# A decoder layer in fp32: modulation blocks that share accumulators, and weight units in pairs

## The chip, the core and the metric

The kernel runs on one core of one Trainium2 chip. The metric is the device time of one launch in microseconds (us), as the median of several runs. A core has a matrix engine (PE, with its weight loads shown apart as PEld), a vector engine (DVE), a scalar engine (ACT), GpSimd (POOL), and SyncE (SP), whose queue issues the weight transfers here. Each engine runs its own list of instructions in the order in which it was written, and semaphores tie the lists together.

## The reference

One layer of a decoder works on a prompt of 256 rows and on 8 x 4 sample rows, together T = 288 rows of D = 2048, all in fp32. A vector c for the prompt and one for each of the 8 samples (9 in all) gives the modulation:

```
sh_m, sc_m, gt_m, sh_f, sc_f, gt_f = split(silu(c) @ w_ada + b_ada, 6)
h = rmsnorm(x) * (1 + sc_m) + sh_m
q, k, v, gu, gv = split(h @ w_in)
merged = concat(rmsnorm(window_attention(q, k, v)), rmsnorm(gelu(gu) * mix(rmsnorm(gelu(gv)))))
x = x + gt_m * rmsnorm(merged @ w_out)
h = rmsnorm(x) * (1 + sc_f) + sh_f
x = x + gt_f * rmsnorm(square(relu(h @ w_ff1)) @ w_ff2)
```

`w_ada` is 2048 x 12288, `w_in` 2048 x 3328, `w_out` 2048 x 2048, `w_ff1` 2048 x 8192 and `w_ff2` 8192 x 2048. The keys, the values and the normalised rows of gv of the sample are outputs too.

## The kernel before

Activations lie transposed, features on the partitions. Each fp32 operand of a big product is the sum of two parts, h (the value rounded to the engine's shorter type) and l (the rest). A weight tile of 128 x 2048 raw values (1 MB) is loaded by SP (L306) into one of 5 buffers, ACT makes its h (CAST, L317) and DVE its l (L318), each in halves of 1024 columns. A product of 128 output columns (`Main`) is then 48 matmuls of 128 x 288: xh and xl against h (L332, L333) and xh against l (L336), twice over 8 tiles of the contraction. `Win` does the same for `w_in` (L478, L479, L481), but in seven groups of the contraction (`KG` of 1, 1, 2, 2, 2, 3 and 5 tiles), because only the part of h that has its modulation can be multiplied; after each group every column tile goes from PSUM to SBUF, by copies in the first group (L486 on ACT, L488 on DVE), by additions on DVE later (L490). `SlabK` (L897) holds several accumulators open and goes along the contraction.

`modnorm` makes one tile of the modulated input: for the 256 prompt rows one DVE instruction with the scale (L283), one ACT instruction with the shift that writes xh (L287) and one on DVE that writes xl (L289); for the 32 sample rows three small DVE instructions (L284, scale L285, shift L286), a CAST on ACT (L288) and xl (L291). `prep(g)` calls it for the tiles of group g ahead of the products of that group.

The modulation is worked out in 96 units of 1 MB of `w_ada`, which stand in 34 blocks (which of the six vectors, first tile, width w of 1, 2 or 4 tiles). A unit (`Ada.run`, L359) multiplies a 128 x 32 slice of the activated c (9 columns and zeros) with the raw weights in fp32, 16 / w matmuls that go around the four 32-row strips of one PSUM bank; each shows as two matmuls in the profile. After the last unit of a block, ACT copies the bank (adS, L363), `ada_fin` makes w transposes on PE (L371), and DVE reduces over the four strips (L373) and adds the bias (L381); a scale or gate is also multiplied with a gain (L383).

What sets the order: the items are written into one list, and `drive` runs it, loading 4 units ahead and splitting 1 ahead. `spread` mixes the ada units of group g+1 between the products of group g. In the attention the tables `NA_L` and `NA_A` say how many units `na` puts after each step, between the slabs of the output projection it is `NA_S`, between its products `NA_O`, and `NA_R` units are left for the residual. In the feed-forward stage the last vector (`Gf`) has one item of `adas2` after each product of the first layer with c > 0. A scheduler then sorts the instructions of each engine by priority and readiness, so that the true order of an engine is that of the built program, not of the list.

Of the kernel before, what the change touches and what calls it, by code (L numbers as in the profile page):

```python
# [62 lines left out]
def _order():  # L63
    res = []
    for g in range(len(KG)):
        res += _mix_blocks(g)
    res += [(2, 4 * q, 4) for q in range(4)]
    for q in range(4):
        res += [(4, 4 * q, 4), (3, 4 * q, 4)]
    return res + [(5, 4 * q, 4) for q in range(4)]  # L70


ADA_BLOCKS = _order()
# [32 lines left out]
def build():  # L106
# [32 lines left out]
    with tile.TileContext(nc) as tc, ExitStack() as root:  # L139
# [37 lines left out]
        cT = cp.tile([128, KT, 9], F32, name="cT")  # L177
# [4 lines left out]
        ones2 = cp.tile([128, 128], F32, name="ones2")  # L182
        eps = cp.tile([128, 1], F32, name="eps")
        mods = {n: cp.tile([128, KT, 9], F32, name="mod_" + n) for n in ("Am", "Bm", "Gm", "Af", "Bf", "Gf")}

# [10 lines left out]
        V.memset(ones2, 2.0 / D)  # L196
        V.memset(eps, EPS)

        sc = cp.tile([128, KT, 32], F32, name="sc")
# [5 lines left out]
        V.tensor_tensor(sc[:, :, 0:9], sg_, cT, ALU.mult)  # L205
# [12 lines left out]
        def norm_r(ps, name):  # L218
# [3 lines left out]
            exp_ln(r, ps, AF.Ln, bias=eps)  # L222
            V.tensor_scalar(a, ps, EPS, None, ALU.add)  # L223
            rsqrt(r, a, t, False)
            return r

        class Sumsq:
            def __init__(self, n, pe, w=None):
                self.n, self.pe, self.i = n, pe, 0
                self.w = ones if w is None else w  # L230
                if pe:
                    self.ps = pp.tile([128, 512], F32, name="ps")[:, :T]
# [6 lines left out]
            def add_sq(self, sq):  # L239
                if self.pe:  # L240
                    PE.matmul(self.ps, self.w, sq, start=self.i == 0, stop=self.i == self.n - 1)
# [16 lines left out]
            def open(self, stop):  # L258
                self.ps = pp.tile([128, 512], F32, name="ps")[:, :T]
                PE.matmul(self.ps, self.w, self.acc, start=True, stop=stop)  # L260

            def close(self, src):
# [3 lines left out]
                PE.matmul(self.ps, self.w, sq, start=False, stop=True)  # L266
# [75 lines left out]
        class Ada(Unit):  # L342
            nosplit = True

            def __init__(self, blk, i):
                self.c, self.j0, self.w = self.blk = blk
                self.i = i
                self.src = d_wada[ADA_ROW[blk] + i]

            def run(self):  # L350
                w, cw = self.w, 128 * self.w
                if self.i == 0:
                    st["ada", self.blk] = pa.tile([128, 512], F32, name="ada")
                ps = st["ada", self.blk]
                nk = KT // w
                for kk in range(nk):
                    k = self.i * nk + kk
                    g = 32 * (k % 4)
                    PE.matmul(ps[g:g + 32, :cw], sc[:, k], self.raws[:, kk * cw:kk * cw + cw], start=k < 4,  # L359
                              stop=k >= KT - 4, skip_group_check=True)  # L360
                if self.i == w - 1:
                    sb = cp.tile([128, 512], F32, name="adS", bufs=2)
                    S.copy(sb[:, :cw], ps[:, :cw])  # L363
                    st["ada", self.blk] = sb

        def ada_fin(blk):
            c, j0, w = blk
            sb = st["ada", blk]
# [3 lines left out]
            m = cp.tile([128, 4, 9], F32, name="adm", bufs=2)[:, :w]  # L372
            V.tensor_reduce(m, pt[:, :w * 128].rearrange("p (w g c) -> p w c g", w=w, g=4)[:, :, 0:9], AX.X, ALU.add)  # L373
            n = ADA[c]
            dst = mods[n][:, j0:j0 + w]

            def row(name, a):
                o_ = SMALL[name][0] + a
                return small[:, o_:o_ + w].unsqueeze(2).to_broadcast([128, w, 9])

            V.tensor_tensor(m if n in ADG else dst, m, row("bada", 16 * c + j0), ALU.add)  # L381
            if n in ADG:
                V.tensor_tensor(dst, m, row(ADG[n], j0), ALU.mult)  # L383

        def ada_items(blk):
            return [Ada(blk, i) for i in range(blk[2])] + [Do(ada_fin, blk)]
# [24 lines left out]
        # ---- norm of x  # L411
        first = []
        for b in _mix_blocks(0):
# [6 lines left out]
        def norm_x():  # L420
# [6 lines left out]
            st["rx"] = norm_r(s0.result(), "r_x")  # L427

        # ---- small tables
# [20 lines left out]
        # ---- startup: ada for mixing scale / shift and first 12 column tiles of W_in  # L450
# [49 lines left out]
        # ---- attention  # L500
# [136 lines left out]
        # ---- gMLP  # L637
# [87 lines left out]
        # ---- schedule: startup  # L725
        def prep(g):
            for k in range(KG0[g], KG0[g] + KG[g]):
                modnorm(k, st["rx"], mods["Am"], mods["Bm"])

# [12 lines left out]
        for g in range(len(KG) - 1):  # L742
            win = [Win(pc) for pc in WIN_PIECES if pc[0] == g]
            ada = []
            for b in _mix_blocks(g + 1):
                ada += ada_items(b)
            ada.append(Do(prep, g + 1))
            if g == GTAB:
                ada.append(Do(tables))
            if g == GSMP:  # L750
                ada.append(Do(samp0, 0))
            items += spread(win[:-1], ada) + win[-1:]

        def ssq_attn(i):
            if i == 0:
                st["sa"] = Sumsq(8, False, ones2)
            st["sa"].add(at[:, i])

        def rattn():
            st["ra"] = norm_r(st["sa"].result(), "r_a")  # L760

        def ssq_gate(h):
            if h == 0:
                st["sg"] = Sumsq(8, False, ones2)
# [7 lines left out]
        def rgate():  # L772
            st["rg"] = norm_r(st["sg"].result(), "r_g")

        adas = []
        for b in ADA_BLOCKS:
            if b[0] in (2, 3, 4):
                adas += ada_items(b)
        adas2 = []
        for b in ADA_BLOCKS:  # L780
            if b[0] == 5:
# [377 lines left out]
```

## Time and profile before

| | |
|---|---|
| time of the runs | 1332.75, 1334.24, 1335.09 us (median 1334.24) |
| profiled execution | span 1331.0 us |
| PE busy | 1298.7 us (98%) |
| DVE, ACT busy | 739.8 us (56%), 543.6 us (41%) |
| weight transfers | 291.41 MB, mean 219 GB/s |

The span runs from the first to the last instruction of the one profiled execution; the runs' times also hold what lies around it, some 3 us. PE is busy nearly throughout, so the time is first of all a sum of PE's work; where PE is idle, another engine's chain counts. The stages that the text speaks of: the start with the first groups of `w_in` (to 57 us), its groups 2 to 5 (to 188, by rounded limits), the last group with the attention (to 303), the gate and the first slabs of the output projection (to 345), its remaining products (to 453), the residual and the first slabs of the feed-forward part (to 515), and the feed-forward products (to 1314).

### The profile page before, as it was taken

The numbers are of one execution on the slowest core, as the hardware profiler recorded it, in microseconds if no ns is written. First come the engines' busy times: TensorE is split into PE (matmuls) and PEld (weight loads), VectorE is DVE, ScalarE is ACT, GpSimd is POOL, SyncE is SP. The second block draws the span as 40 slices with busy tenths as digits, with TensorE's granted clock in tenths as the row PEclk, the third lists the DMA queues.
The fourth block names the chain that finished last, engine by engine and source line by source line (L and its number), as shares of the span: only waits on it lengthen the run. The fifth ranks groups of instructions, "written<-read, shape, count | busy, mean of one in ns | idle before, by whom it ended". The sixth has DMA issues, their size and how long they took to land.

```text
span 1331.0 us, 23553 instructions
## 1 busy us (share of the span) xinstructions
PE 1298.7 (98%) x9856; PEld 1184.5 (89%) x9856; DVE 739.8 (56%) x1433; ACT 543.6 (41%) x873; POOL 26.5 (2%) x46
## 2 busy tenths in 40 slices
PE   6999999998999999999999999999999999999997
PEld 5788886766788689999999899999999999999996
DVE  6888675658754497443344444444554444554554
ACT  5332243457443265443434443334443333444432
POOL 0200001200000000000000000000000000000000
PEclk9999998999999999999999999999999999999999
DMA  9988976577987766444457675446444544554411
GB/s 361 333 334 299 343 283 232 185 261 282 335 304 277 286 259 209 171 159 159 165 197 268 237 273 191 159 159 253 158 163 167 176 161 159 164 176 168 159 64 72
DMA packets 45755, 291.41 MB, mean 219 GB/s; under 512 B 5578, under 2 KB 6154, under 8 KB 14800
## 3 DMA queue, kind: packets, MB, share of 16 engines
q1 hardware_dynamic: 43344, 284.26, 59.0%
q0 software_dynamic: 2160, 5.47, 1.7%
q8 instruction: 77, 1.26, 0.4%
q14 instruction: 30, 0.25, 0.1%
q10 hardware_dynamic: 144, 0.18, 0.0%
HBM read 287.18 MB, written 2.70 MB: 218 GB/s over the span
## 4 chain that ended last, share of the span: by engine, by line
PE 60%; DVE 1%; ACT 0%; DVEq 0%; issue 0%
PE ps L332 20%; PE ps L336 20%; PE ps L333 19%; PE ada L359 1%; DVE acc L1041 0%; DVE x L1047 0%; PE ada L371 0%; PE ps L1038 0%; ACT nr L166 0%; PE ps L266 0%; PE ps L260 0%; DVE nr L216 0%; DVE mn L215 0%; DVE mn L214 0%; DVE mn L223 0%; DVEq L139 0%
## 5 line engine op out<-in xcount | busy, mean ns | idle before, releaser
L318 DVE TENSOR_TENSOR l<-raw,h 128x1024 fp32r<-128x1024 f32 (+3 forms) x368 | 417.9, 1140 | 363.3 <-ACT h L317 363.1
L317 ACT CAST h<-raw 128x1024 fp32r<-128x1024 f32 (+3 forms) x368 | 359.5, 984 | 581.4 <-PE ps L333 495.6
L332 PE MATMUL ps<-xh,h 128*128 128x288 f32 x1120 | 304.6, 299 | 0.7 <-ACT sq L984 0.7
L333 PE MATMUL ps<-xl,h 128*128 128x288 f32 x1120 | 301.3, 295 | 0.0
L333 PE MATMUL ps<-fl,h 128*128 128x288 f32 x1024 | 276.9, 295 | 0.0
L332 PE MATMUL ps<-fh,h 128*128 128x288 f32 x1024 | 276.9, 298 | 0.0
L332 PEld LDWEIGHTS ps<-xh,h 128*128 128x128 f32 x1120 | 210.5, 188 | 23.6 <-ACT fh L985 12.6
L333 PEld LDWEIGHTS ps<-xl,h 128*128 128x128 f32 x1120 | 211.6, 189 | 0.0
L332 PEld LDWEIGHTS ps<-fh,h 128*128 128x128 f32 x1024 | 193.0, 188 | 0.8 <-ACT fh L985 0.8
L333 PEld LDWEIGHTS ps<-fl,h 128*128 128x128 f32 x1024 | 192.3, 188 | 0.0
L336 PE MATMUL ps<-xh,l 128*128 128x288 f32 x1120 | 171.6, 295 | 0.0
L336 PE MATMUL ps<-fh,l 128*128 128x288 f32 x1024 | 157.3, 296 | 0.0
L336 PEld LDWEIGHTS ps<-xh,l 128*128 128x128 f32 x1120 | 156.1, 188 | 0.0
L336 PEld LDWEIGHTS ps<-fh,l 128*128 128x128 f32 x1024 | 142.7, 188 | 0.0
L478 PE MATMUL ps<-xh,h 128*128 128x288 f32 x416 | 117.9, 306 | 3.7 <-DVE gv L490 2.0
L479 PE MATMUL ps<-xl,h 128*128 128x288 f32 x416 | 117.4, 300 | 0.0
L359 PE MATMUL ada<-raw,sc 128*32 128x512 f32 (+2 forms) x1088 | 108.1, 482 | 8.4 <-DMA raw<-wada 8.4
L478 PEld LDWEIGHTS ps<-xh,h 128*128 128x128 f32 x416 | 77.6, 190 | 18.4 <-issue 6.3
L481 PE MATMUL ps<-xh,l 128*128 128x288 f32 x416 | 86.0, 299 | 0.0
L479 PEld LDWEIGHTS ps<-xl,h 128*128 128x128 f32 x416 | 79.2, 191 | 2.7 <-issue 2.4
L481 PEld LDWEIGHTS ps<-xh,l 128*128 128x128 f32 x416 | 65.9, 190 | 0.9 <-issue 0.8
L359 PEld LDWEIGHTS ada<-raw,sc 128*32 128x32 f32 x1088 | 29.6, 112 | 37.9 <-issue 32.3
(250 smaller groups left out, 949.9 us busy)
## 6 DMA issues: line engine op xcount, KB each, us to landing
raw<-wada SPq DMA_DIRECT2D x96, 1024.0 KB, 6.7
raw<-f SPq DMA_DIRECT2D x64, 1024.0 KB, 4.8
raw<-f1B SPq DMA_DIRECT2D x58, 1024.0 KB, 4.8
raw<-woB SPq DMA_DIRECT2D x12, 1024.0 KB, 6.8
raw<-win SPq DMA_DIRECT2D x11, 1024.0 KB, 9.2
raw<-win SPq DMA_DIRECT2D x14, 640.0 KB, 5.1
raw<-f1A SPq DMA_DIRECT2D x8, 768.0 KB, 6.0
raw<-win SPq DMA_DIRECT2D x6, 768.0 KB, 6.0
```

What stands on the lines that cost most here:

```text
L317: S.copy(h, rw)
L318: V.tensor_tensor(l, rw, h.bitcast(F32), ALU.subtract)
L332: PE.matmul(ps, w, self.mh[:, k], start=k == 0, stop=False)
L333: PE.matmul(ps, w, self.ml[:, k], start=False, stop=False)
L336: PE.matmul(ps, l[:, kk * 128:kk * 128 + 128], self.mh[:, k], start=False, stop=k == 15)
L359: PE.matmul(ps[g:g + 32, :cw], sc[:, k], self.raws[:, kk * cw:kk * cw + cw], start=k < 4, stop=k >= KT - 4, skip_group_check=True)
L478: PE.matmul(ps, w, xh[:, k0 + kk], start=kk == 0, stop=False)
L479: PE.matmul(ps, w, xl[:, k0 + kk], start=False, stop=False)
L481: PE.matmul(ps, l[:, o_ + kk * 128:o_ + kk * 128 + 128], xh[:, k0 + kk], start=False, stop=kk == s - 1)
```

## The change

Blocks of `w_ada` now stand in sets. A set of up to three blocks of the same width shares one accumulator: c stands 18 columns from the left in a zeroed tile 50 columns wide, and block n of a set multiplies with the 32 columns from 18 - 9 n on, so that its 9 rows land at 9 n. One copy, w transposes and one reduction then serve the whole set; the additions and multiplications stay one per block. For the mixing part the sets are pairs of scale and shift (9 sets of 2), for the gate Gm and the second part's scale and shift 4 sets of 3, for Gf sets of 3 and 1: 15 copies and reductions instead of 34, 40 transposes instead of 96. The matmuls of the units are as many as before (544 in the program).

The units stand in pairs: `pairs` groups them for `spread` and for the feed-forward stage, the tables have even numbers, and after every second product of the output projection stand two units. `NA_O` and `NA_R` are gone. Besides, c lies in the tile that later holds Af, the second constant of ones is replaced by a scale in `norm_r`, and `adm` has one wider buffer instead of two.

```
-NA_L = (0, 2, 1, 3, 3, 0, 2)
-NA_A = (1, 1, 1, 1, 1, 1)
-NA_O, NA_R = 13, 8
-NA_S = (0, 0, 1, 1, 2, 2, 2, 2)
+NA_L = (0, 2, 0, 4, 4, 0, 2)
+NA_A = (2, 0, 2, 0, 2, 0)
+NA_S = (0, 0, 2, 0, 2, 2, 2, 2)
...
+        mix.append([b[i:i + 2] for i in range(0, len(b), 2)])
...
+    return (mix, [ff[i:i + SHARE] for i in range(0, len(ff), SHARE)],
+            [gf[i:i + SHARE] for i in range(0, len(gf), SHARE)])
...
+        c0 = 9 * (SHARE - 1)
+        sc = cp.tile([128, KT, c0 + 32], F32, name="sc")
...
+                nk, s0 = KT // w, c0 - 9 * self.n
                 for kk in range(nk):
                     k = self.i * nk + kk
                     g = 32 * (k % 4)
-                    PE.matmul(ps[g:g + 32, :cw], sc[:, k], self.raws[:, kk * cw:kk * cw + cw], start=k < 4,
-                              stop=k >= KT - 4, skip_group_check=True)
-                if self.i == w - 1:
+                    PE.matmul(ps[g:g + 32, :cw], sc[:, k, s0:s0 + 32], self.raws[:, kk * cw:kk * cw + cw],
+                              start=self.n == 0 and k < 4, stop=self.last and k >= KT - 4, skip_group_check=True)
+                if self.i == w - 1 and self.last:
                     sb = cp.tile([128, 512], F32, name="adS", bufs=2)
                     S.copy(sb[:, :cw], ps[:, :cw])
...
+            ms = cp.tile([128, 4, 9 * SHARE], F32, name="adm", bufs=1)[:, :w, :nb]
+            V.tensor_reduce(ms, pt[:, :w * 128].rearrange("p (w g c) -> p w c g", w=w, g=4)[:, :, 0:nb], AX.X, ALU.add)
+            for i, (c, j0, _) in enumerate(blocks):
+                m = ms[:, :, 9 * i:9 * i + 9]
...
+            ada = pairs(ada)
+            ada[-1].append(Do(prep, g + 1))
...
+            for it in spread([[w] for w in win[:-1]], ada) + [win[-1:]]:
+                items += it
...
             items.append(Main(d_woB[n - NO], xh, xl, ev_o(n)))
-            items += na((n - NO + 1) * NA_O // (16 - NO) - (n - NO) * NA_O // (16 - NO))
-        items += na(len([it for it in adas if it.src is not None]) - NA_R)
+            if (n - NO) % 2:
+                items += na(2)
...
+        adas2 = pairs(adas2)
...
-                if c > 0 and adas2:
-                    items.append(adas2.pop(0))
+                if c > 0 and j % 2 and adas2:
+                    items += adas2.pop(0)
```

The built program shows the order at three places. On DVE, ahead of the very first products of `w_in`: mn, nr, xl and xh are the steps of `modnorm`, adm and mod_Am belong to the modulation, l is a weight's second part, kT and at are evicted column tiles. Before:

```order
L283 SCALAR_TENSOR_TENSOR mn<-x,mod_Am,nr 128x256
L284 TENSOR_TENSOR mn<-x,nr 128x32 x2
L285 TENSOR_TENSOR mn<-mn,mod_Am 128x32
L286 TENSOR_TENSOR mn<-mn,mod_Bm 128x32
L373 TENSOR_REDUCE adm<-ada 128x9
L289 SCALAR_TENSOR_TENSOR xl<-mn,mod_Bm,xh 128x256
```

And now (the lines of after are 5 to 8 further down):

```order
L288 SCALAR_TENSOR_TENSOR mn<-x,mod_Am,nr 128x256
L323 TENSOR_TENSOR l<-raw,h 128x1024 x2
L289 TENSOR_TENSOR mn<-x,nr 128x32
L294 SCALAR_TENSOR_TENSOR xl<-mn,mod_Bm,xh 128x256
L290 TENSOR_TENSOR mn<-mn,mod_Am 128x32
L289 TENSOR_TENSOR mn<-x,nr 128x32
L291 TENSOR_TENSOR mn<-mn,mod_Bm 128x32
```

Two halves of l now stand between the large and the small steps of the first tile.

On DVE again, ahead of the last group of `w_in`, from the reduction whose result that group's first tile needs. Before, with the scale and its product mn done earlier, the shift alone:

```order
L373 TENSOR_REDUCE adm<-ada 128x36
L318 TENSOR_TENSOR l<-raw,h 128x640
L381 TENSOR_TENSOR mod_Bm<-adm,small 128x36
L490 TENSOR_TENSOR gu<-ps,gu 128x288
L286 TENSOR_TENSOR mn<-mn,mod_Bm 128x32 x2
```

Now scale and shift come out of one reduction:

```order
L379 TENSOR_REDUCE adm<-ada 128x4x18
L389 TENSOR_TENSOR adm<-adm,small 128x4x9
L389 TENSOR_TENSOR mod_Bm<-adm,small 128x36
L498 TENSOR_TENSOR gu<-ps,gu 128x288
L323 TENSOR_TENSOR l<-raw,h 128x640 x2
L391 TENSOR_TENSOR mod_Am<-adm,small 128x36
L498 TENSOR_TENSOR gu<-ps,gu 128x288
L288 SCALAR_TENSOR_TENSOR mn<-x,mod_Am,nr 128x256
L290 TENSOR_TENSOR mn<-mn,mod_Am 128x32
L288 SCALAR_TENSOR_TENSOR mn<-x,mod_Am,nr 128x256
L291 TENSOR_TENSOR mn<-mn,mod_Bm 128x32
```

Between the reduction and the first tile's small step with the shift stood three other instructions before; now there are ten.

On PE, in the feed-forward stage, between two products of the first layer. Before, a product's end, one unit, the next product:

```order
L332 MATMUL ps<-xh,h 128x288
L333 MATMUL ps<-xl,h 128x288
L336 MATMUL ps<-xh,l 128x288 x8
L359 MATMUL ada<-raw,sc 32x512 x4
L332 MATMUL ps<-xh,h 128x288
L333 MATMUL ps<-xl,h 128x288
```

Now, after every second product:

```order
L337 MATMUL ps<-xh,h 128x288
L338 MATMUL ps<-xl,h 128x288
L341 MATMUL ps<-xh,l 128x288 x8
L365 MATMUL ada<-raw,sc 32x512 x8
L337 MATMUL ps<-xh,h 128x288
L338 MATMUL ps<-xl,h 128x288
```

Two units stand in one piece. Over the whole program PE's list has 66 such pieces of unit matmuls instead of 83, and 15 pieces of transposes instead of 35.

## Rows read from the trace of the kernel before

**Rows 1.** The page, part 1 (busy time) and part 5 (unit matmuls).

```profile
PE 1298.7 (98%) x9856; PEld 1184.5 (89%) x9856; DVE 739.8 (56%) x1433; ACT 543.6 (41%) x873; POOL 26.5 (2%) x46
...
L359 PE MATMUL ada<-raw,sc 128*32 128x512 f32 (+2 forms) x1088 | 108.1, 482 | 8.4 <-DMA raw<-wada 8.4
```

**Rows 2.** Windows by stage: length, PE, PEld, DVE, ACT, POOL busy, clock, DMA, GB/s.

```profile
0.00:57.00 57.00, 44.81 (x403) 35.78 (x404) 40.91 (x112) 24.97 (x49) 3.67 (x11) 0.97 0.92 347
57.00:188.00 131.00, 130.44 (x1143) 112.64 (x1142) 99.70 (x247) 44.19 (x75) 7.97 (x13) 1.00 0.88 327
188.00:303.00 115.00, 114.09 (x845) 83.45 (x844) 68.18 (x207) 47.50 (x151) 13.31 (x20) 0.94 0.65 227
303.00:345.00 42.00, 36.59 (x241) 23.67 (x240) 39.26 (x141) 29.32 (x68) 1.50 (x3) 1.00 0.79 292
345.00:453.00 108.00, 108.00 (x801) 92.83 (x799) 51.08 (x94) 37.03 (x52) 0.00 (x0) 1.00 0.77 287
453.00:515.00 62.00, 58.07 (x406) 47.66 (x405) 52.34 (x147) 36.08 (x69) 0.00 (x0) 1.00 0.77 287
515.00:1314.00 799.00, 799.00 (x5997) 783.00 (x5998) 376.90 (x472) 320.75 (x402) 0.00 (x0) 1.00 0.50 174
```

**Rows 3.** Timeline of PE: start, length, line, tiles; products, units, transposes.

```profile
358.34 1.92 PE L359 MATMUL ada<-raw,sc 128*32 128x512 f32 x16
360.20 0.40 PE L332 MATMUL ps<-xh,h 128*128 128x288 f32 x1
...
366.76 1.07 PE L359 MATMUL ada<-raw,sc 128*32 128x512 f32 x8
...
518.28 0.29 PE L332 MATMUL ps<-xh,h 128*128 128x288 f32 x1
...
521.46 0.29 PE L332 MATMUL ps<-xh,h 128*128 128x288 f32 x1
...
739.68 1.06 PE L359 MATMUL ada<-raw,sc 128*32 128x512 f32 x8
...
747.24 1.07 PE L359 MATMUL ada<-raw,sc 128*32 128x512 f32 x8
...
754.71 0.60 PE L371 MATMUL ada<-small,adS 128*128 128x128 f32 x4
...
761.60 0.64 PE L359 MATMUL ada<-raw,sc 128*32 128x512 f32 x4
```

**Rows 4.** Timeline of the start, on PE, DVE and ACT.

```profile
22.12 1.10 PE L478 MATMUL ps<-xh,h 128*128 128x288 f32 x4 [1.01 <-ACT xh L288]
...
54.34 0.40 PE L478 MATMUL ps<-xh,h 128*128 128x288 f32 x1 [1.96 <-DVE gv L490]
...
20.78 0.48 DVE L283 SCALAR_TENSOR_TENSOR mn<-x,mod_Am,nr 128x256 f32<-128x256 f32 x1
...
50.59 2.34 DVE L318 TENSOR_TENSOR l<-raw,h 128x1024 fp32r<-128x1024 f32 x2
...
21.85 0.22 ACT L288 CAST xh<-mn 128x32 fp32r<-128x32 f32 x1
```

**Rows 5.** Timeline ahead of the last group of `w_in`, DVE and PE.

```profile
179.05 0.31 DVE L373 TENSOR_REDUCE adm<-ada 128x36 f32<-128x144 f32 x1 [0.51 <-PE ada L371]
180.11 0.45 DVE L490 TENSOR_TENSOR gu<-ps,gu 128x288 f32<-128x288 f32 x1
...
181.30 0.80 PE L478 MATMUL ps<-xh,h 128*128 128x288 f32 x4 [0.56 <-ACT xh L288]
```

**Rows 6.** Timeline of PE and a window, around the sample attention.

```profile
188.51 1.04 PE L359 MATMUL ada<-raw,sc 128*32 128x512 f32 x2
...
220.00:234.00 14.00, 14.00 (x78) 9.46 (x78) 1.74 (x4) 0.96 (x2) 1.72 (x3) 0.51 0.48 155
```

**Rows 7.** Timeline of PE: transposes, and the first slab after the residual.

```profile
305.18 0.66 PE L371 MATMUL ada<-small,adS 128*128 128x128 f32 x4 [0.71 <-ACT adS L363]
...
475.08 1.06 PE L897 MATMUL ps<-xh,h 128*128 128x288 f32 x6 [0.51 <-ACT xh L288]
```

More of the change, by code (lines that the diff above doesn't have):

```diff
@@ L216, in rsqrt, with norm_r @@
             V.scalar_tensor_tensor(dst, t, 1.5, dst, ALU.add, ALU.mult)
-        def norm_r(ps, name):
+        def norm_r(ps, scale=1.0):
             a = cp.tile([128, T], F32, name="mn", bufs=3)
@@ L227, in build, with __init__ @@
         class Sumsq:
-            def __init__(self, n, pe, w=None):
+            def __init__(self, n, pe):
                 self.n, self.pe, self.i = n, pe, 0
-                self.w = ones if w is None else w
                 if pe:
@@ L240, in add_sq @@
                 if self.pe:
-                    PE.matmul(self.ps, self.w, sq, start=self.i == 0, stop=self.i == self.n - 1)
+                    PE.matmul(self.ps, ones, sq, start=self.i == 0, stop=self.i == self.n - 1)
                 elif self.i == 0:
@@ L259, in open @@
                 self.ps = pp.tile([128, 512], F32, name="ps")[:, :T]
-                PE.matmul(self.ps, self.w, self.acc, start=True, stop=stop)
+                PE.matmul(self.ps, ones, self.acc, start=True, stop=stop)
             def close(self, src):
@@ L265, in close @@
                 S.activation(sq, src, AF.Square)
-                PE.matmul(self.ps, self.w, sq, start=False, stop=True)
+                PE.matmul(self.ps, ones, sq, start=False, stop=True)
                 self.pe = True
@@ L343, in build, with __init__ @@
             nosplit = True
[L345 to L348, printed above, removed]
+            def __init__(self, blocks, n, i):
+                self.c, self.j0, self.w = self.blk = blocks[n]
+                self.key, self.n, self.i, self.last = blocks[0], n, i, n == len(blocks) - 1
+                self.src = d_wada[ADA_ROW[self.blk] + i]
             def run(self):
                 w, cw = self.w, 128 * self.w
[L352 to L355, printed above, removed]
+                if self.i == 0 and self.n == 0:
+                    st["ada", self.key] = pa.tile([128, 512], F32, name="ada")
+                ps = st["ada", self.key]
+                nk, s0 = KT // w, c0 - 9 * self.n
                 for kk in range(nk):
@@ L371, in ada_fin, with row, ada_items @@
                 PE.transpose(pt[:, q * 128:q * 128 + 128], sb[:, q * 128:q * 128 + 128], ident)
[L372 to L386, printed above, removed]
+            ms = cp.tile([128, 4, 9 * SHARE], F32, name="adm", bufs=1)[:, :w, :nb]
+            V.tensor_reduce(ms, pt[:, :w * 128].rearrange("p (w g c) -> p w c g", w=w, g=4)[:, :, 0:nb], AX.X, ALU.add)
+            for i, (c, j0, _) in enumerate(blocks):
+                m = ms[:, :, 9 * i:9 * i + 9]
+                n = ADA[c]
+                dst = mods[n][:, j0:j0 + w]
+                def row(name, a):
+                    o_ = SMALL[name][0] + a
+                    return small[:, o_:o_ + w].unsqueeze(2).to_broadcast([128, w, 9])
+                V.tensor_tensor(m if n in ADG else dst, m, row("bada", 16 * c + j0), ALU.add)
+                if n in ADG:
+                    V.tensor_tensor(dst, m, row(ADG[n], j0), ALU.mult)
+        def ada_items(blocks):
+            return [Ada(blocks, n, i) for n, b in enumerate(blocks) for i in range(b[2])] + [Do(ada_fin, blocks)]
         class Do(Unit):
@@ L412, in build @@
         first = []
-        for b in _mix_blocks(0):
+        for b in MIX_SETS[0]:
             first += ada_items(b)
@@ L728, in prep, with pairs @@
                 modnorm(k, st["rx"], mods["Am"], mods["Bm"])
+        def pairs(its):
+            out = []
+            for it in its:
+                if it.src is None:
+                    out[-1].append(it)
+                elif out and len(out[-1]) == 1:
+                    out[-1].append(it)
+                else:
+                    out.append([it])
+            return out
         def spread(a, b):
```

69 lines of the change are left out of this document (32 added, 37 removed).

## The prediction

> **What bounds the kernel now.** I read the page first, then windows by stage, then PE's timeline inside a stage. PE is busy for 1298.7 of 1331.0 us [rows 1], so time is gained where PE's own work shrinks, or where a wait ahead of PE goes. The windows tell the two kinds of stage apart [rows 2]. From 345 to 453 us and from 515 to 1314 PE is busy for all 108.00 and 799.00 us: an edit there is worth what it takes from PE. From 303 to 345 PE works for 36.59 of 42.00 us while DVE has 39.26, and from 453 to 515 for 58.07 of 62.00 with DVE at 52.34: there a chain through DVE and ACT sets the end, and less work on PE buys little. From 57 to 188 PE is nearly full (130.44 of 131.00) but DVE has 99.70, so that little cover stands between a modulation and its products. Only this stage and the start can lose much.
>
> **Prices.** Two neighbouring halves of a product start at 518.28 and 521.46, so a product takes 2 x 3.18 = 6.36 us. From one unit to the next with a product between are 747.24 - 739.68 = 7.56 us: a lone unit costs 1.20. Two units in one piece and a product take 366.76 - 358.34 = 8.42: the pair costs 2.06, which is 0.34 less than two lone ones. From 747.24 to 761.60 lie two products, a unit and four transposes: 14.36 - 12.72 - 1.20 = 0.44, or 0.11 a transpose, much less than the 0.60 that the row shows as its length, since neighbours overlap [rows 3]. All matmuls of the units stay (108.1 us of PE time [rows 1]), and so do their transfers.
>
> **Part by part**, in us against the profiled span of 1331.0.
>
> 1. *Start to the second group.* +2.6, between 0 and +5.5. The first product waits for xh, whose last 32 columns the CAST of 21.85 writes; the product follows at 22.12 [rows 4]. In the new order of DVE two halves of l stand between the first large step (20.78) and the small steps that the CAST needs. Two such halves take 2.34 [rows 4], a reordered xl step a little more: the first product starts some 2.5 later. At the next group the scale comes out of the same transposes as the shift, so a multiplication, a large step of 0.48 and some small ones are added to the chain, +1.5 with what stands beside them. Given back: before, PE stands still for 1.96 at 54.34, since the eviction of gv waits on DVE behind two l halves (50.59, 2.34) [rows 4]; a later start finds these done, and I take back 1.4. The lower bound says that all is given back, the upper that nothing is, and that a wait of 1.5 is added ahead of group 2. The second load of `w_in` is moved ahead of a unit's load on SP's queue, which is why those halves can be ready so early; it costs the unit one slot, and that unit has no reader until later.
>
> 2. *Groups 2 to 6* (57 to 188). 12 transposes less, -1.3; 18 pieces of units instead of 23, 5 x 0.34 = -1.7. Against it, new waits: scale and shift now come out of one reduction, and behind it stand the additions, the multiplication, the large step and the small ones before the group's first product can start. In the last group the row before shows the shortest form: reduction at 179.05, first product at 181.30 after 0.56 of idle [rows 5]. New in that chain are one more l half (640 columns of 1024 at 1.17: 0.73), one more eviction (0.45 [rows 5]), two large steps (0.48 [rows 4]) and two small ones (about 0.2): 2.5 by lengths, and 2.0 since neighbours overlap. In groups 3 to 5 PE's list leaves 2.9 to 3.4 us of products and units behind the transposes, and the chain is some 3.6: 0.75, 0.4 and 0.3. Sum of the waits 3.45, of the part +0.4; between -3.0 (no new wait) and +5.2 (2.05 in each of four groups).
>
> 3. *Last group and attention* (188 to 303). The tables put two units in most places, but the scheduler cuts them: 13 pieces in place of 11, with lengths such as 1 and 3 matmuls. A single one takes 1.04, as much as a unit of four (1.06) [rows 3, 6], because four strips work side by side. Rounded up to fours, pieces at 0.34 and fours at 0.86 (the second unit of a pair, 2.06 - 1.20) make +1.5. One unit is moved in from the output projection, +1.2; two groups of four transposes less, -0.9. Together +1.8, from 0 to +3.5.
>
> 4. *Gate and first slabs* (303 to 345). Of two groups of four transposes one goes (0.44); each waited for an adS copy, the first for 0.71 [rows 7]. -1.0, and 0 to -2 as bounds, with the rest of the wait held by DVE [rows 2].
>
> 5. *Output projection* (345 to 453). 5 pairs x 0.34 = -1.7; two groups of transposes, -0.9; the unit that went to part 3, -1.2. -3.8; PE is full here, so it all counts. If the scheduler splits a pair I lose 0.34 a piece.
>
> 6. *Residual* (453 to 515). One group of transposes leaves the slabs, -0.4. The others, and their copies, stood beside the sums of squares, which wait for DVE and ACT; the first slab waits for xh as before (0.51 [rows 7]). From -1.0 to +1.0.
>
> 7. *Feed-forward.* 8 pairs in place of 16 lone units, 8 x 0.34 = -2.7; two groups of transposes less, -0.9. -3.6. The copies and reductions that go were hidden behind products (ACT and DVE are busy for 320.75 and 376.90 of 799.00 us [rows 2]) and count for nothing.
>
> At nothing I put: the wider zeroed tile and the one constant less (written while the loads of x are under way), c in the tile of Af (first written after c is used up), one `adm` buffer less (writer and readers stand in order on DVE).
>
> Sum: 2.6 + 0.4 + 1.8 - 1.0 - 3.8 - 0.4 - 3.6 = -4.0. The span comes to 1327.0; the median of the runs lies 3.2 above the profiled span, so the time is 1330.3.
>
> A rule of the Trainium skill speaks against part 1. The row shows that gv's eviction, due on DVE, waited until two l halves were through, and PE 1.96 us for it [rows 4]. TensorE: Matmul & The Clock Gate (the table it opens with, queue depth) says that the vector and scalar engines take their lists strictly in order, and only the matrix engine may pull weight loads ahead. By it the small steps wait for both halves; could DVE pass them, part 1 would be nearly nothing, and the time 1327.7. The row agrees with the rule.
>
> **Rivals.**
>
> (a) *No new waits.* The halves of l come when DVE is idle anyway, and the chains fit behind PE's work. For it: before, no group from the third to the fifth makes PE wait (0.56 of idle in all from 57 to 188 [rows 2]). Then part 1 and the 3.45 go: -4.0 - 2.6 - 3.45 = -10.0, 1324.2.
>
> (b) *Pairs save nothing.* The 0.34 rests on one pair at 358.34, behind a slab and not a product [rows 3]. If it belongs to that place, parts 2, 5 and 7 lose 1.7 + 1.7 + 2.7: +2.1, 1336.4.
>
> (c) *Slower: every group waits for its joint chain.* Place: the reduction ahead of each of the groups 2 to 6. Price 2.6 each (2.05 and the idle 0.56 that the last group has already) and 5.5 at the start, 18.5 in place of 6.05: -4.0 + 12.4 = +8.4, 1342.7. For it: DVE's 99.70 us in 131 [rows 2], where the chain joins a queue. Against it: groups 3 to 5 have other products behind their transposes. It decides for slower from 12.7 us of such waits on, as the rest saves 10.0 and 2.7 are needed.
>
> (d) *The slow stretch goes.* From 220 to 234 PE has a granted clock of 0.51 [rows 6], its 1.2 GHz level, after many small matmuls of the sample attention; elsewhere it is 1.00. Now twice as many unit matmuls stand right before that part, and one among its small ones. If the clock stays up, 14.0 x 0.49 = 6.9 go: 1323.4. The Trainium skill says in TensorE: Matmul & The Clock Gate (Part 1: The HAM clock gate) that a block which watches how busy the engine has been of late grants the clock. By this rule more filler could keep 2.4 GHz; the row agrees as to the place, but shows a fall while PE was counted as busy.
>
> (e) *A second slow stretch* opens in the second half of the sample attention, where a filler is moved away: 10 us at half the clock, +5.0, 1335.3.
>
> **How the numbers follow.** This kernel's runs tell 0.2% (2.7 us) from no change: faster means below 1331.6, slower above 1336.9. The forecast has 0.50, (a) 0.16, (b) 0.11, (c) 0.11, (d) 0.07, (e) 0.05. Within the forecast the bounds of parts 1 to 3 alone spread some 3 us to either side; 1330.3 lies only 1.3 under the line, so I count 0.33 of its 0.50 as faster and 0.17 as the same. Faster: 0.33 + 0.16 + 0.07 = 0.56. The same: 0.17 + 0.11 + 0.05 = 0.33. Slower: 0.11. The range reaches from (d), 1323.0, to the edge of (b) and the upper bounds of parts 1 and 2, 1337.0; what lies beyond is (c) and a tail below.
>
> **What would show it.** In the changed profile the first product of `w_in` should start near 24.6 after a wait for the CAST, and the second group's near 58. PE should wait for xh ahead of group 6 for about 2.6 us, with waits under 1 us at groups 3 to 5. In the feed-forward stage two units and their neighbours should take 2.06 over the products' 6.36. Six pairs or so and one group of transposes should stand between the products of the output projection, which should be 3.8 shorter. The clock should fall once, for about 14 us near 220. I am wrong if the first product starts at 22 to 23, if a pair costs 2.4, or if groups 3 to 5 wait for over 2 us each.

## The result, and the profile after

The changed kernel takes 1341.08 us (median of 4 runs, 1338.62 to 1343.03) where the kernel before takes 1334.52; the ratio is 1.0052 with an interval of 1.0041 to 1.0064. It is slower, by some 7 us; the forecast was 1330.3 us, and its range ended at 1337.0. The profiled execution took 1343.03 us, its span is 1341.3, 10.3 longer than the span before. It was the slowest of its four runs and the profiled one before the fastest of its four, so the profiles lie 10.3 us apart where the medians lie 6.6 apart.

The page after, first line of part 1, answers to the first of [rows 1]:

```profile
PE 1296.9 (97%) x9800; PEld 1186.7 (88%) x9800; DVE 737.4 (55%) x1413; ACT 536.9 (40%) x854; POOL 26.5 (2%) x46
```

PE has less to do than before (9800 matmuls instead of 9856) and is yet busy for nearly as long. To see why, both kernels are cut at the same places of the program: the first product of group 2 of `w_in` (counted from 0, so the third; the prediction calls it the second), the first matmul of the attention, the first sum of squares of its output, the first product of the output projection, its sum of squares, the first feed-forward product, and the last sum of squares. The windows of the kernel before (length, then busy time of PE, PEld, DVE, ACT and POOL, PE's granted clock, DMA share, GB/s):

```profile
0.00:55.64 55.64, 43.45 (x392) 34.42 (x393) 39.55 (x108) 24.97 (x49) 2.41 (x8) 0.97 0.92 344
55.64:189.49 133.85, 133.29 (x1158) 114.49 (x1157) 102.55 (x255) 44.91 (x76) 9.79 (x16) 1.00 0.88 325
189.49:300.97 111.48, 110.57 (x825) 81.04 (x825) 65.45 (x200) 45.46 (x147) 12.76 (x19) 0.94 0.65 227
300.97:360.20 59.23, 53.82 (x369) 38.19 (x367) 51.00 (x165) 38.56 (x86) 1.50 (x3) 1.00 0.82 301
360.20:453.05 92.85, 92.85 (x691) 80.24 (x687) 40.58 (x72) 29.10 (x37) 0.00 (x0) 1.00 0.75 280
453.05:514.98 61.93, 58.00 (x405) 47.64 (x405) 52.32 (x147) 36.06 (x69) 0.00 (x0) 1.00 0.77 287
514.98:1314.47 799.49, 799.49 (x6001) 783.49 (x6002) 376.93 (x472) 320.77 (x402) 0.00 (x0) 1.00 0.50 174
```

and those of the changed kernel, which answer to [rows 2]:

```profile
0.00:61.01 61.01, 45.49 (x389) 35.62 (x389) 39.96 (x104) 25.97 (x48) 5.09 (x13) 0.94 0.86 328
61.01:197.33 136.32, 133.84 (x1156) 115.42 (x1153) 100.51 (x248) 42.39 (x69) 7.09 (x12) 0.99 0.82 313
197.33:313.78 116.45, 110.58 (x820) 79.94 (x817) 64.92 (x199) 44.90 (x145) 13.37 (x20) 0.94 0.69 231
313.78:376.81 63.03, 55.96 (x361) 40.51 (x359) 50.37 (x160) 38.30 (x82) 0.99 (x2) 0.92 0.71 271
376.81:465.83 89.02, 89.02 (x675) 79.42 (x671) 40.48 (x73) 27.36 (x37) 0.00 (x0) 1.00 0.74 283
465.83:529.10 63.27, 59.11 (x398) 47.88 (x397) 52.69 (x145) 34.93 (x67) 0.00 (x0) 0.97 0.77 281
529.10:1324.79 795.69, 795.69 (x5992) 782.91 (x5993) 377.08 (x470) 319.25 (x400) 0.00 (x0) 1.00 0.50 175
```

A window gives its length and PE's idle time, which is length less busy time. The clock's part is read from the stretches that PE ran at its 1.2 GHz level. A product's matmul starts there every 0.24 us, and every 0.1325 us elsewhere (24 in 3.18 us [rows 3]), so 0.45 of PE's busy time in such a stretch is what the clock costs; the trace after has both paces side by side:

```profile
30.06 0.44 PE L487 MATMUL ps<-xl,h 128*128 128x288 f32 x1
30.30 0.44 PE L489 MATMUL ps<-xh,l 128*128 128x288 f32 x1
...
31.18 0.29 PE L487 MATMUL ps<-xl,h 128*128 128x288 f32 x1
31.31 0.30 PE L489 MATMUL ps<-xh,l 128*128 128x288 f32 x1
```

What is left of a change in length is a change in PE's work. Change from before to after, in us:

| stage | length | idle | clock | work |
|---|---|---|---|---|
| start and first groups | +5.4 | +3.3 | +0.9 | +1.1 |
| groups 2 to 5 | +2.5 | +1.9 | +1.5 | -1.0 |
| last group and attention | +5.0 | +5.0 | 0.0 | 0.0 |
| gate and slabs | +3.8 | +1.7 | +3.9 | -1.8 |
| output projection | -3.8 | 0.0 | 0.0 | -3.8 |
| residual and slabs | +1.3 | +0.2 | +1.3 | -0.2 |
| feed-forward | -3.8 | 0.0 | 0.0 | -3.8 |
| sum | +10.3 | +12.1 | +7.7 | -9.4 |

(Sums are of unrounded terms. The work of the start is uncertain by some 1 us: two programs below that leave its code as before come out at -1.0 and -0.8 there.) The work that was to be saved is saved, 9.4 us. Against it stand 12.1 us of new waits of PE, and 7.7 from the clock: new stretches in which PE is granted its 1.2 GHz level. Most of them lie right behind a new wait. PE's waits over 1.5 us in the timeline after, from 20 us to the feed-forward stage, with the idle time and what ended it in brackets (one of 1.17 at 319.32 is the next longest):

```profile
21.55 0.81 PE L365 MATMUL ada<-raw,sc 128*32 128x128 f32 x18 [2.63 <-DMA raw<-wada]
25.33 0.61 PE L486 MATMUL ps<-xh,h 128*128 128x288 f32 x1 [2.96 <-ACT xh L293]
...
186.52 0.80 PE L486 MATMUL ps<-xh,h 128*128 128x288 f32 x4 [1.82 <-ACT xh L293]
...
228.22 0.33 PE L629 MATMUL ps<-small,Ls 128*128 128x128 f32 x1 [2.35 <-DVE Ls L620]
...
294.20 0.40 PE L486 MATMUL ps<-xh,h 128*128 128x288 f32 x1 [2.40 <-ACT h L322]
...
353.20 1.89 PE L365 MATMUL ada<-raw,sc 128*32 128x512 f32 x2 [3.95 <-DMA raw<-wada]
...
488.69 1.81 PE L917 MATMUL ps<-xh,h 128*128 128x288 f32 x6 [1.73 <-ACT xh L293]
```

and the low stretches ahead of the tail, after (with the window behind the wait of 294.20) and then before, the clock being the third number from the end of a line and PE's busy time the second number:

```profile
23.95:30.78 6.83, 5.45 (x23) 5.45 (x24) 2.97 (x12) 1.72 (x5) 0.00 (x0) 0.50 0.82 295
187.79:191.21 3.42, 3.42 (x16) 3.42 (x15) 3.31 (x12) 1.22 (x4) 0.00 (x0) 0.50 0.60 247
228.75:232.16 3.41, 3.41 (x11) 1.00 (x10) 0.00 (x0) 0.62 (x2) 0.00 (x0) 0.50 0.99 413
235.58:245.82 10.24, 10.24 (x56) 6.93 (x55) 1.50 (x4) 0.96 (x2) 1.79 (x3) 0.50 0.28 40
294.00:297.00 3.00, 2.80 (x25) 2.04 (x29) 2.82 (x9) 2.62 (x9) 0.32 (x1) 1.00 0.89 357
320.91:324.32 3.41, 3.41 (x17) 3.41 (x16) 3.41 (x16) 3.40 (x4) 0.00 (x0) 0.50 0.99 417
351.63:358.46 6.83, 5.26 (x14) 3.34 (x15) 2.34 (x10) 1.55 (x3) 0.00 (x0) 0.50 0.37 150
488.17:491.58 3.41, 2.89 (x12) 2.89 (x13) 3.41 (x12) 3.36 (x8) 0.00 (x0) 0.50 0.63 253
...
22.42:25.83 3.41, 3.41 (x16) 3.41 (x16) 1.86 (x8) 2.34 (x4) 0.00 (x0) 0.50 1.01 404
220.39:234.05 13.66, 13.66 (x76) 9.18 (x74) 1.74 (x4) 0.96 (x2) 1.76 (x3) 0.50 0.47 148
```

Busy time in them is 34.07 us after and 17.07 before; 0.45 of the difference is the 7.7. With five waits (186.52, 228.22, 319.32, 353.20 and 488.69) there comes a low stretch, right behind the wait or beginning within it; with that of 294.20 there comes none. The stretch of the sample attention (235 to 246) is there before too [rows 6], and shorter now. In the kernel before, with its waits of 1.96 at 54.34 [rows 4] and 0.51 at 475.08 [rows 7], there are but these two.

The runs of one program differ by the clock as well: the four of the changed kernel took 1338.62, 1340.77, 1341.39 and 1343.03 us at mean clocks of 0.988, 0.986, 0.984 and 0.985. The kernel before, run beside the experiments below, shows 0.989 to 0.994, so the clock's part is not that of the profiled execution alone.

### The profile page after: what moved, and what is told of

It reads as the page before. It is cut to its first block, busy times and chain, and to the rows that moved or that the text cites. A ratio compares the mean times of both kernels' runs of the same rounds, so it can differ in the third digit from the quotient of the medians.

```text
span 1341.3 us, 23386 instructions
## 1 busy us (share of the span) xinstructions
PE 1296.9 (97%) x9800; PEld 1186.7 (88%) x9800; DVE 737.4 (55%) x1413; ACT 536.9 (40%) x854; POOL 26.5 (2%) x46
## 4 chain that ended last, share of the span: by engine, by line
PE 59%; DVE 1%; ACT 0%; DVEq 0%; issue 0%
PE ps L337 20%; PE ps L341 19%; PE ps L338 19%; PE ada L365 1%; DVE acc L1062 0%; DVE x L1068 0%; PE ps L1059 0%; PE ada L377 0%; ACT nr L173 0%; PE ps L271 0%; PE ps L265 0%; DVE mn L220 0%; DVE mn L221 0%; DVE nr L222 0%; DVE mn L229 0%; DVEq L146 0%
```

## Experiments

Three theories of the loss are tried: **P**, that pairs do it; **S**, that the sets do; and **H**, that a wait of PE costs more than itself, since the clock falls behind it. In the table, ratios are to the kernel before on the same chip, with the 95% interval; the other columns are worked out as above, against the profile before and without the tail. They are those of one profiled execution each, and the clock's part changes from run to run.

| kernel | median us | ratio | length | idle | clock | work |
|---|---|---|---|---|---|---|
| changed kernel | 1341.08 | 1.0052 (1.0041 to 1.0064) | +10.3 | +12.1 | +7.7 | -9.4 |
| sets alone | 1338.07 | 1.0037 (1.0016 to 1.0058) | +9.5 | +8.4 | +9.8 | -8.7 |
| pairs alone | 1340.84 | 1.0055 (1.0034 to 1.0076) | +9.1 | +7.3 | +4.8 | -2.9 |
| both, from the gates' sets on | 1337.01 | 1.0027 (1.0013 to 1.0041) | +3.9 | +5.3 | +7.1 | -8.4 |
| both, mixing part alone | 1345.74 | 1.0093 (1.0071 to 1.0115) | +17.0 | +9.2 | +6.4 | +1.4 |
| late pairs | 1329.44 | 0.9967 (0.9955 to 0.9980) | -3.4 | +0.6 | +2.5 | -6.5 |
| wait probe | 1364.72 | 1.0236 (1.0222 to 1.0250) | +33.2 | +22.6 | +9.4 | +1.2 |
| changed, old tables | 1343.65 | 1.0077 (1.0060 to 1.0094) | +8.0 | +10.5 | +7.2 | -9.7 |
| feed-forward alone | 1329.13 | 0.9968 (0.9956 to 0.9980) | -2.6 | -0.2 | +1.5 | -3.9 |
| changed, lone start | 1336.99 | 1.0022 (1.0011 to 1.0033) | +3.6 | +12.7 | +2.4 | -11.5 |
| changed, old slabs | 1341.10 | 1.0056 (1.0029 to 1.0083) | +10.2 | +12.7 | +6.8 | -9.4 |
| waits filled | 1359.26 | 1.0197 (1.0180 to 1.0214) | +27.0 | +6.1 | +2.9 | +18.0 |

**Sets alone.** The items by the rules of the kernel before:

```diff
-            ada = pairs(ada)
-            ada[-1].append(Do(prep, g + 1))
+            ada.append(Do(prep, g + 1))
+            ada = [[it] for it in ada]
...
-NA_L = (0, 2, 0, 4, 4, 0, 2)
+NA_L = (0, 2, 1, 3, 3, 0, 2)
...
-        adas2 = pairs(adas2)
+        adas2 = [[it] for it in adas2]
```

> The shared accumulators alone: sets as in the changed kernel, but lone units in the places and by the tables of the kernel before. Theory P (the loss comes from units in pairs: two neighbours hold two of the five raw buffers until both are used, so that the loads behind them come late): start and attention as before, fewer transposes and copies, about 1330 us, the first product of w_in's third group near 55.5 to 57 us. Theory S (the loss comes from the sets: scale and shift out of one reduction make a longer chain ahead of each group): the 6.8 us that start and groups lost stay, some 3.5 us of transposes go, about 1338 us.

Measured: slower, 1.0037. The start is delayed by 1.8 us, not by the 5.4 of the changed kernel (first product at 21.77, group 2 at 57.46), so its larger part belongs to the pairs. But gate and slabs are 6.8 longer, with this wait for a unit's load ahead of the output projection, the same as at 353.20 above:

```profile
344.90 1.92 PE L365 MATMUL ada<-raw,sc 128*32 128x512 f32 x2 [3.98 <-DMA raw<-wada]
```

Neither P nor S alone: the sets lose at the gate, the pairs at the start.

**Pairs alone.** Each block its own set:

```diff
-        mix.append([b[i:i + 2] for i in range(0, len(b), 2)])
+        mix.append([[q] for q in b])
...
-    return (mix, [ff[i:i + SHARE] for i in range(0, len(ff), SHARE)],
-            [gf[i:i + SHARE] for i in range(0, len(gf), SHARE)])
+    return (mix, [ff[i:i + 1] for i in range(0, len(ff), 1)],
+            [gf[i:i + 1] for i in range(0, len(gf), 1)])
```

> Pairs alone: every block keeps its own accumulator, copy, transposes and reduction; units in pairs and the tables of the changed kernel. Theory P: late loads at the start (+5), in the attention (+5) and at the gate (+4), less 1.7 in the output projection and 2.7 in the feed-forward stage, about 1343 us. Theory S: none of these, only the gain of pairs, about 1331 us.

Measured: slower, 1.0055. The start is 7.7 us longer, the attention 5.1 (4.5 of it PE's work: by the timeline 13 pieces of units instead of 9, with one unit and one group of transposes more), gate and slabs 1.9, with a wait of 1.67 for a unit's load at 350.54. The output projection and the feed-forward stage gain 2.9 each. P holds for the start.

**Both, from the gates' sets on.** The mixing blocks alone and lone, the tables of before, the rest as changed.

> Both edits from the output projection on and in the sets of Gm, Af, Bf and Gf; the mixing part's blocks and the tables of attention and gate as in the kernel before. If the gains of the stages in which PE is full are worth what the trace shows (3.8 and 3.8 us), about 1327 us, faster than both kernels. If they come back as waits elsewhere (residual, clock), about 1334 us.

Measured: slower, 1.0027. The gains are there (-3.5 and -3.8), but the sets of Gm, Af and Bf give them back: gate and slabs +3.2, residual +5.8. In the residual PE comes to the set's four transposes while their copy still stands on ACT behind the first steps of the next modulated tiles, and the clock behind it is low:

```profile
479.05 0.66 PE L377 MATMUL ada<-small,adS 128*128 128x128 f32 x4 [3.66 <-ACT adS L369]
481.00 0.61 PE L917 MATMUL ps<-xh,h 128*128 128x288 f32 x1 [1.29 <-ACT h L322]
...
480.00:487.00 7.00, 6.00 (x25) 6.00 (x26) 7.00 (x19) 4.10 (x7) 0.00 (x0) 0.51 0.60 214
```

**Both, mixing part alone.** The sets of scale and shift in pairs, all else as before.

> Both edits for the mixing part's scale and shift alone; all blocks of Gm, Af, Bf and Gf, the tables and the later stages as in the kernel before. If the 6.8 us lost by the last group's start are made there (joint chains or late loads, both theories), about 1341 us; if they belong to what follows (the tables of the attention), about 1335 us.

Measured: the slowest, 1.0093. Start +7.5, groups +2.0, attention +5.8 (2.3 idle, 3.1 clock), gate and projection 0.0, residual +1.7. The mixing part is where both edits lose at once.

**Changed, old tables.**

```diff
-NA_L = (0, 2, 0, 4, 4, 0, 2)
-NA_A = (2, 0, 2, 0, 2, 0)
-NA_S = (0, 0, 2, 0, 2, 2, 2, 2)
+NA_L = (0, 2, 1, 3, 3, 0, 2)
+NA_A = (1, 1, 1, 1, 1, 1)
+NA_S = (0, 0, 1, 1, 2, 2, 2, 2)
```

> The changed kernel with the tables of the kernel before for attention and gate (sets, pairs elsewhere as changed). If the 8.8 us that attention and gate lost come from where the new tables put units (blocks of four ahead of the sample's scores, two units at a time between slabs, whose loads come late), they go: about 1333 us. If they come from the sets, or are passed on from the late start, about 1341 us stay.

Measured: no faster (1.0077). The attention's loss goes from 5.0 to 0.6 us, so that one is the tables'; the sample's scores still wait, for 2.36. Gate and slabs keep 3.0, and the residual now loses 4.7, for the same copy as above. The sets hold there, whatever the table.

**Changed, old slabs.** Only `NA_S` set back.

> The changed kernel with the table of the kernel before for the units between slabs (NA_S) alone. If the wait of 3.95 us for a unit's load ahead of the output projection, and the low clock behind it, come from that table, gate and slabs are some 5 us shorter: about 1336 us. If they come from the sets, which leave no transposes between the units of three blocks so that PE comes to a unit whose load is still under way, the wait stays: 1341.

Measured: no change against the changed kernel (1.0056). The wait for a unit's load ahead of the projection is 2.3 us instead of 3.95, gate and slabs are 2.7 longer than before instead of 3.8, and the start came out 2.3 longer than in the changed kernel with the same order. The rival holds by and large: the sets, not that table.

**Changed, lone start.** Lone units in the first group's stretch alone:

```diff
-            ada = pairs(ada)
+            ada = pairs(ada) if g else [[it] for it in ada]
```

> The changed kernel with lone units (sets still shared) between the products of the first group of w_in alone. The second load of w_in then stands behind a unit's load again, and on DVE the two halves of l behind the small steps of the first tile. If the pair is what delays the start, the first product starts near 22 us instead of 25.3 and the second group's products near 58 (the joint chain's share, +2, stays) instead of 61: some 3 us less than the changed kernel in the start, about 1338 in all, less or more by how often the clock falls later. If the sets delay it, no change: 1341.

Measured: 1336.99, 1.0022. The first product starts at 23.00, group 2 at 58.50, as expected. But the groups behind lose 4.1, so that at the attention's start the kernel is 7.0 late against 7.8. What makes it faster is above all the clock, which costs 2.4 instead of 7.7; idle is +12.7 against +12.1, work -11.5 against -9.4, most of that in the start, where it is uncertain. Why its waits bring fewer low stretches is not shown. All its seven runs have mean clocks of 0.987 to 0.991, the four of the changed kernel 0.984 to 0.988.

**Wait probe.** Seven waits where PE has none, in the kernel before:

```diff
+            with tc.high_priority(offset=200):
+                t = cp.tile([128, T], F32, name="sq", bufs=3)
+                S.activation(t, st["lastps"], AF.Identity, scale=0.0)
+                for _ in range(n - 1):
+                    S.activation(t, t, AF.Identity, scale=0.0)
+                for k in (0, 8):
+                    S.activation(xh[:, k, 0:1], xh[:, k, 0:1].bitcast(F32), AF.Identity, bias=t[:, 0:1])
```

> The kernel before with seven waits of PE put into the feed-forward stage, where it has none: after a product a chain of 1, 2, 3, 4, 5, 7 and 10 small ACT instructions on its result, whose last adds zero to two columns of xh that the next product reads. By chain links of 0.45 us and 0.9 us around them the waits should be 1.3 to 5.4 us, 20 us in all. Theory H (a wait of PE is followed by a stretch at 1.2 GHz, which costs some 1.7 us more, or 3.4): 20 + 12 us or more above the kernel before, with stretches of a low clock right behind most waits, and products there at half speed. Rival: a wait costs itself alone, 20 us, the clock 1.00 in the whole stage.

Measured: +32 us. In the trace the waits are 1.31, 1.79, 2.26, 2.74, 3.21, 4.16 and 5.59 us, 21.1 in all; the feed-forward stage is 31.2 longer. Behind five of the seven the clock falls. Windows behind the first four, the sixth and the seventh wait (behind the fifth the clock is 0.67):

```profile
948.00:951.00 3.00, 3.00 (x23) 3.00 (x24) 0.73 (x2) 0.71 (x2) 0.00 (x0) 1.00 0.73 218
975.00:979.00 4.00, 3.67 (x17) 3.67 (x18) 0.70 (x2) 0.47 (x2) 0.00 (x0) 0.61 0.74 260
1005.00:1009.00 4.00, 4.00 (x31) 4.00 (x32) 0.62 (x1) 1.05 (x1) 0.00 (x0) 1.00 0.69 262
1136.00:1139.00 3.00, 3.00 (x16) 3.00 (x15) 0.00 (x0) 0.00 (x0) 0.00 (x0) 0.54 0.71 300
...
1197.00:1201.00 4.00, 3.52 (x15) 3.52 (x16) 0.00 (x0) 0.58 (x3) 0.00 (x0) 0.59 0.45 188
1230.00:1236.00 6.00, 5.74 (x26) 5.75 (x27) 0.00 (x0) 1.44 (x3) 0.00 (x0) 0.56 0.01 3
```

The first and the third wait cost themselves alone, the second (1.79 us) does not. H holds, not for every wait: of the 10.1 us that the stage loses beyond the waits, the low clock behind the five costs 8.4.

**Waits filled.** The same chains, and matmuls while they run:

```diff
+                for q in range(m):
+                    PE.matmul(ps2, xl[:, 3, 0:128], xh[:, 3], start=q == 0, stop=q == m - 1)
```

> The seven chains of the wait probe, with 8 to 30 extra matmuls of the same shape into an unread PSUM tile between the product and the wait, so that PE works while each chain runs (122 matmuls by 0.1325 us, 16.2 of the 21 us of waits; what is left of each wait is 0.3 to 1.6 us). The products still start as late as in the wait probe. If idle PE lets the clock fall (theory H), the clock stays 1.00 there and the 10 us beyond the 21 go: about 1354 us where the wait probe took 1364.7. If the products' late start or the ACT chains bring the low clock, 1364 stays.

Measured: 1359.26. In the built order each block of extra matmuls came one wait early, so that it filled the six shorter waits (what was left of them was 0.23 us or less) and left the seventh, of 5.59 us, open. That makes it a cleaner comparison: the clock is 1.00 over all six filled waits, and falls behind the one that is still idle.

```profile
517.00:1210.00 693.00, 692.44 (x5189) 675.10 (x5188) 313.06 (x370) 283.92 (x377) 0.00 (x0) 1.00 0.52 180
...
1224.00:1228.00 4.00, 3.08 (x13) 3.08 (x14) 0.00 (x0) 0.99 (x4) 0.00 (x0) 0.57 0.17 72
```

The stage is 25.3 us longer than before, against 31.2 with the waits open, though its products start as late (and one block more of eight matmuls is worked through). All its four runs have a mean clock of 0.989 or 0.990, all four of the wait probe 0.984. So it is PE's idleness behind which the clock falls, not the late start nor the chains on ACT.

**Late pairs, and feed-forward alone.** Two versions that leave all stages with waits as they were. The first has pairs between the products of the output projection (three units in the first place, so that pairs end with blocks) and both edits for Gf; the second only the latter.

```diff
-            if (n - NO) % 2:
-                items += na(2)
+            if (n - NO) % 2:
+                items += na(3 if n == NO + 1 else 2)
```

> The kernel before up to the output projection, with the residual's order as there; pairs between the products of the output projection and of the feed-forward stage, and shared accumulators for Gf alone. No new wait should arise, as PE is full in both stages: 3.8 us less in the feed-forward stage and 1.7 to 2.0 in the output projection, 5.5 us below the kernel before (about 1327.5 where that has 1333), the mean clock unchanged. If gains in full stages are given back (by the clock, or by waits later), no change.

> The kernel before with pairs and shared accumulators for Gf in the feed-forward stage alone: 3.8 us less than the kernel before, all of it in that stage (8 x 0.34 and two groups of four transposes), nothing elsewhere. Rival: another clock or other waits before that stage move the time by as much.

Measured: 0.9967 and 0.9968, faster than both kernels. The feed-forward stage of both, and in between the output projection of the first:

```profile
515.38:1311.07 795.69, 795.69 (x5993) 782.91 (x5994) 377.28 (x470) 319.37 (x400) 0.00 (x0) 1.00 0.50 175
...
362.34:453.45 91.11, 91.11 (x690) 80.50 (x686) 40.23 (x73) 27.84 (x38) 0.00 (x0) 1.00 0.74 286
...
516.22:1311.91 795.69, 795.69 (x5992) 782.91 (x5993) 377.25 (x470) 319.59 (x400) 0.00 (x0) 1.00 0.50 175
```

Each feed-forward stage has become 3.80 us shorter, the output projection 1.74. In both profiles the sample attention's low stretch lasts 17.1 us instead of 13.7, and its stage is 1.6 longer with 0.1 of idle, which hides part of the gain there; by the price above those 3.4 us cost 1.5. The medians do not tell the two versions apart: the first's 1.7 us lie within what the runs differ by (1327.03 to 1329.54, and 1328.39 to 1330.45).

## Why the prediction was wrong

**Prices and full stages: right.** A pair with its two products takes 722.73 - 707.98 = 14.75 us after, 2.03 above two products (2.06 forecast):

```profile
707.98 0.64 PE L365 MATMUL ada<-raw,sc 128*32 128x512 f32 x4
...
722.73 0.64 PE L365 MATMUL ada<-raw,sc 128*32 128x512 f32 x4
```

Part 5 forecast -3.8 and got -3.83, part 7 forecast -3.6 and got -3.80. All that I counted as PE's work came to -10.0, and -9.4 was measured. That the sums are so near is in part luck: groups 2 to 5 saved 1.0 where 3.0 was forecast, the attention took nothing more where 1.8 was forecast, and the gate saved 1.8 where its whole part was -1.0. Rival (b) is out.

**Part 1: the mechanism, but half the size** (forecast +2.6, at most +5.5; measured +5.4). The two halves of l stand where the order put them (21.84 for 2.35 us on DVE), and the first product starts at 25.33 instead of the forecast 24.6. The step that failed is the giving back: 1.4 us were to return, since before PE waits for 1.96 at 54.34 [rows 4]. After, PE waits there for 0.95 and 0.80 (the profile puts the latter down to a load, but in three programs with the same start to an eviction on DVE), 1.75 in all, and the loss stays at +5.4, of which 0.9 is the clock's. That the pair does it, by moving the loads and with them DVE's halves, is shown by the lone start (23.00) and by the sets alone (21.77): in both, DVE has the small steps ahead of the halves again. The size is less sure: with the start as changed, group 2 begins between 59.52 and 63.35 in four programs.

**Part 2: about right in the waits.** The wait ahead of the last group is 1.82 us (forecast 2.6), that of group 4 0.58, of groups 3 and 5 under 0.1. Rival (c) came near the time (1342.7), but by a mechanism that did not happen: the groups did not all wait for their joint chains.

**Parts 3 and 4: wrong.** I counted transposes and pieces there, and no wait. Attention and gate lost 5.0 and 3.8 us. In the attention the sample's scores wait on DVE (2.35), and a product for its load (2.40); the old tables took 4.4 of the 5.0 away, the wait for the load among it, but not that of the scores. At the gate the wait that I wanted to remove (0.71 [rows 7]) is still there, and 3.95 for a unit's load has come. That the sets are enough to bring it is shown: the sets alone, with lone units and the old tables, wait for 3.98, the changed kernel with the old tables for 3.17, and where Gm, Af and Bf keep their own blocks and tables (both edits in the mixing part alone) units there wait for loads for 0.4 us in all. They are not the only way to it, as the pairs alone wait there for 1.67. Why PE comes to that unit ahead of its load is only argued: without transposes and copies between three blocks it has less to do on the way. Part 4 had as its bounds 0 and -2, so a loss was left out without a reason; a stage in which DVE and ACT are as busy as PE [rows 2] was the last place for that. The opening said that only the start and groups 2 to 5 could lose much; attention, gate and residual lost 10.1 together. In the residual (part 6, +1.3 against bounds of -1.0 and +1.0) PE's wait ahead of the first slab grew from 0.51 [rows 7] to 1.73 (shorter ones went, idle is +0.2 in all), and the clock behind it costs the 1.3.

**The clock: a term put at nothing.** Rivals (d) and (e) looked for the clock in the sample attention alone, and (d) says that it is 1.00 elsewhere, though [rows 2] has 0.97 for the start: PE is at its 1.2 GHz level from 22.42 on, behind waits of 1.31 and 1.01. What I missed is that each new wait of PE can bring a low stretch of its own, wherever it stands. I had 6.05 us of new waits in the sum, at their own length. There were 12.1, and 7.7 of clock. Without the clock's part the sum would have been +2.7, at the edge of no change; with the waits at the forecast size as well, -3.4, near the -4.0 of the forecast. So two steps failed: the waits were counted at half of what they are, which turns the sign, and the clock behind them was put at nothing, which makes most of the size. The Trainium skill says in TensorE: Matmul & The Clock Gate (Part 1: The HAM clock gate) that the clock follows how busy the engine has lately been. I weighed that for more filler, as a gain; the same rule speaks of every wait, as a loss. The wait probe agrees with it (31.2 us for 21.1 of waits), and so does the filled one.

**Profiled execution and median.** I added 3.2 us to the span, the distance to the median. The profiled execution itself was the run of 1332.75, so its own surroundings are 1.75; the rest was that it was the fastest of three runs. (And 1327.0 and 3.2 make 1330.2, not 1330.3.)

What stays open is which wait brings a fall. One of 1.79 us did and one of 2.26 did not, in the same stage. One and the same wait of the start (54.34 in [rows 4]) is followed by a fall in three profiled executions, of both edits from the gates' sets on, of the feed-forward alone and of the filled waits, and by none in three, of the kernel before, of the late pairs and of the wait probe. The feed-forward alone, and below it the kernel before:

```profile
52.56 0.40 PE L486 MATMUL ps<-xh,h 128*128 128x288 f32 x1 [1.96 <-DVE gv L498]
53.00:57.00 4.00, 4.00 (x21) 4.00 (x20) 2.88 (x8) 1.26 (x2) 2.94 (x6) 0.57 1.02 430
...
55.00:59.00 4.00, 4.00 (x33) 4.00 (x32) 3.39 (x10) 1.26 (x2) 3.27 (x7) 1.00 1.01 426
```

So the length of a wait and its place do not settle it, and the clock's part of a forecast can only be a range.

## What to carry to other kernels

A wait of PE is to be priced with what the clock does behind it: here 1.5 us in most cases, 2.2 behind the longest, and now and then nothing. So work that is taken from PE is a gain where PE is full on both sides of the edit, and in a stage with chains it is one only if what stood there did not also cover a chain; an edit of both kinds is best made in the full stages alone, which here turned +0.5% into -0.3%. Items that stand in pairs also pair their loads and their buffers: look at what the second load pushes back.

## What was not expected of the hardware

Waits of 1.8 to 5.6 us in a stage that was otherwise full brought PE down to 0.54 to 0.67 of its clock in the windows behind them, five times of seven, at a cost of some 1.5 us each and 2.2 behind the longest. Runs of one program differ along with it: ten runs of the sets alone took from 1333.21 us at a mean clock of 0.992 to 1345.20 at 0.983, where the kernel before stayed between 1330.90 and 1336.31 in 19 runs. A single unit matmul in a piece of its own takes 1.04 us as before [rows 6], which fits the cost of the pieces that the scheduler cuts (work +4.5 in the attention of the pairs alone).
